# Thirteen prepared pairs, a fifth pair by seven products, and another order of DVE's and the transfers' work in an up projection

## The chip, the cores and the metric

The kernel runs on one core of one Trainium2 chip. The metric is the device time of one execution in microseconds (us); the time of a version is the median of its runs. Engines are called as in the profile: PE (TensorE's matmuls), PEld (its weight loads), DVE (VectorE), ACT (ScalarE), POOL (GpSimd), SP (SyncE, which only queues transfers here).

## The reference, cut to what matters

One decoder layer for 256 positions of width 2048: a projection, two kinds of attention (8 + 8 heads), an output projection, and an MLP with a hidden width of 8192. The change lies in the first half of the MLP.

```python
x = x + _rmsnorm(mixed @ w_out[layer], norm_attn_post[layer])
h = _rmsnorm(x, norm_mlp_pre[layer])
u = jnp.square(jax.nn.relu(h @ w_up[layer]))
x = x + _rmsnorm(u @ w_down[layer], norm_mlp_post[layer])
```

Everything is float32, `h` is 256 x 2048, `w_up` 2048 x 8192, `w_down` 8192 x 2048.

## The kernel before, in words

**Products.** A float32 operand is split into two float32r parts: `hi` (a rounded copy, by ACT, `split` L306 or with a gain L310) and `lo` (what is left, by DVE, L307 or L311). A product of two operands is three matmuls of 128 x 128 by 128 x 512 (`three`: hi·hi, hi·lo, lo·hi).

**Weights.** All weight tiles of the kernel stand in one list (`weights.plan`). A tile is 128 x 1024 at most. `weights.get(i)` emits the work on the tiles up to `i + 6`: a load by SP into one of 5 buffers `raw`, then the split into one of 8 pairs of buffers `hi` and `lo`; `weights.free(i)` gives tile `i`'s buffers back. `weights.first[i]` holds functions that are called just before tile `i` is made. So what they queue stands on its engine's queue between the work of tiles `i - 1` and `i`, some six tiles ahead of PE.

**The up projection** runs in 8 chunks `j` of 1024 columns. A chunk has 16 rows of tiles `k` (128 rows of `w_up` each). `UP_STEPS[j]` gives its order: a step `k` is one tile, 12 matmuls (2 blocks of 128 positions, 2 halves of 512 columns, 3 each). A step `p` or `w` is a pair of rows, `2k` and `2k + 1`, done as a 2 x 2 block product by Winograd's seven products in place of eight (`seven_products`): 21 matmuls and not 24. For it the weights' side needs sums of the pair's four blocks:

- In a `w` pair DVE makes them. POOL queues two transfers of the pair into the tile `ab` (`load_two`, L374), and DVE adds (`seven`: L359, L363, L364) into `t` and `u`. These additions (`sums`) are called `SUMS_AHEAD` = 2 tiles ahead of the pair's first tile, and no sooner than the last `w` pair's tiles are planned. Then four tiles are split: half of `a`, then `b`, `u`, `t`.
- In a `p` pair the sums lie in HBM, made by transfers alone while the front of the kernel runs (`prepare`, L577 to L584: two copies by SP, then four accumulating transfers by POOL; the flow below starts one pair every 24 us). They are loaded like weights, by SP into `raw`.

The left side's sums, of `hT`, are made once for each pair (`left_sums`), by DVE and ACT; with them `hT` itself gets its gain, so later chunks split these rows' weights without one (`SCALED`).

At the end of a chunk's pairs, `close` combines four accumulators `m` (PSUM banks) into four tiles `c` in SBUF: one copy by ACT (L1052), four operations by DVE (L1055). The banks of `m` are those of the next chunk's accumulators. `up_evac` then runs for each of the chunk's four quarters: DVE adds `c` to the accumulator (L954), ACT applies relu with a scale (L957), PE transposes (L300, tile `rt`), ACT squares into `uT` (L971).

**Order.** The program is emitted by hand in one order. `Flow` keeps a modelled clock that each matmul moves on by 0.216 us; generators such as `up_evac`, `left_sums` and `prepare_all` yield delays, and `flow.pump()`, called after each group of three matmuls, emits the steps that are due. Every engine works through its own part of that order. So a `yield` sets not a time but the place of an instruction in its engine's queue.

Of the kernel before, what the change touches and what calls it, by code (L numbers as in the profile page):

```python
# [18 lines left out]
F32 = mybir.dt.float32  # L19
F32R = mybir.dt.float32r  # L20
# [3 lines left out]
OP = mybir.AluOpType  # L24
PSUM = bass.MemoryType.PSUM

P = 128
# [65 lines left out]
D_UP, UP_STEP = 1.8, 2.2  # L93


SUMS_AHEAD = 2
NUP = FF // CW


def steps_of(text):  # L100

    return [(s[0], int(s[1:])) for s in text.split()]


UP_STEPS = {0: [("k", k) for k in range(KD)]}
for _j in range(1, 6):
    UP_STEPS[_j] = steps_of("k8 k9 k10 k11 p0 k12 w1 k13 w2 p3 k14 k15")
for _j in range(6, NUP):
    UP_STEPS[_j] = steps_of("k6 k7 k8 k9 k10 w0 k11 k12 w1 k13 w2 k14 k15")
SCALED = {j: range(8) for j in range(1, NUP)}  # L110
PREP = [(j, k) for j in UP_STEPS for w, k in UP_STEPS[j] if w == "p"]
D_PREP = (50.0, 24.0, 12.0)

# [53 lines left out]
class Weights:  # L167
# [15 lines left out]
    def load(self, src, w, name, queue=None):  # L183
        raw = self.pool.tile([P, CW], F32, tag="raw", bufs=RAW_BUFS, name=name)
        out = raw[:, :w]
        if len(src.shape) == 3:
            out = out.rearrange("p (k n) -> p k n", k=src.shape[1])
        (queue or self.nc.sync).dma_start(out=out, in_=src)
        return raw
# [74 lines left out]
def layer(nc, tc, io):  # L264
# [38 lines left out]
    def split(hi, lo, src, g=None):  # L303
        if g is not None:
            return split_gain(hi, lo, src, g)
        nc.scalar.activation(hi, src, AF.Copy)  # L306
        nc.vector.tensor_tensor(out=lo, in0=src, in1=hi.bitcast(F32), op=OP.subtract)  # L307
# [33 lines left out]
    def up_weight(j, k):  # L341
        return io["w_up"][k * P:(k + 1) * P, j * CW:(j + 1) * CW]
# [4 lines left out]
    def seven(load, targets):  # L347

        st, tt, H = {}, nc.vector.tensor_tensor, 512

        def sums():
            ab = load()
            a, b = st["a"], st["b"] = [ab[:, :CW], ab[:, CW:]] if not isinstance(ab, list) else ab
            t, u = st["t"], st["u"] = targets()
            if not isinstance(ab, list):
                two = [x.rearrange("p (k n) -> p k n", n=H) for x in (t, ab)]
                tt(out=two[0], in0=two[1][:, 0:2, :], in1=two[1][:, 1:4:2, :], op=OP.add)  # L359
            else:  # L360
                for x, o in ((a, 0), (b, H)):
                    tt(out=t[:, o:o + H], in0=a[:, o:o + H], in1=x[:, H:], op=OP.add)
            tt(out=u[:, :H], in0=t[:, :H], in1=b[:, H:], op=OP.add)  # L363
            tt(out=u[:, H:], in0=u[:, :H], in1=b[:, :H], op=OP.add)  # L364

        def b11(hi, lo):
            split(hi[:, :H], lo[:, :H], st["a"][:, :H])

        return sums, [b11] + [lambda hi, lo, n=n: split(hi, lo, st[n]) for n in "but"]

    def load_two(raw, queue, src):
        for i in range(2):
# [29 lines left out]
        st, left[c, kp] = down_parts(c, kp)  # L402
        nc.gpsimd.dma_start(out=st.bitcast(F32), in_=skeep[kp])

    def plan_seven(sums, fs, after, more=(), last=()):

        at = max(len(weights.specs) - SUMS_AHEAD, after)
        for n, f in (*more, (0, sums), *((0, f) for f in last)):
            weights.first.setdefault(at - n, []).append(f)
        return [weights.plan(f) for f in fs], len(weights.specs)  # L410

    wide_u, after = [], 0
    for j in range(NUP):
        wide_u.append([])
        for what, k in UP_STEPS[j]:
            if what == "k":
                g = () if k in SCALED.get(j, ()) else (gcol[:, 8 + k:9 + k],)
                ts = [weights.plan(up_weight(j, k), 1, CW, *g)]  # L420
            elif what == "p":
                kept = sums_kept[j, k]
                ts = [weights.plan(src, 1, n) for src, n in (
                    (up_weight(j, 2 * k)[:, :512], 512), (up_weight(j, 2 * k + 1), CW),
                    (kept[:, CW:], CW), (kept[:, :CW], CW))]
            else:
                ts, after = plan_seven(*seven_up(j, k), after)
            wide_u[j].append((what, k, ts))

    def down_weight(c, k):  # L430
# [518 lines left out]

    def up_evac(j, b, i, acc, order, more=None):  # L950

        yield UP_STEP * order
        if more is not None:
            nc.vector.tensor_tensor(out=acc, in0=acc, in1=more, op=OP.add)  # L954
            yield 1.6
        r = late["up"].tile([P, 512], F32, tag="r", bufs=2, name=f"r{j}_{b}")
        nc.scalar.activation(r, acc, AF.Relu, scale=rstd2[b])  # L957
        yield D_UP if j > 1 else 2 * D_UP
        t = bank(i, f"rt{j}_{b}")
        for k in range(4):  # L960
            transpose(t[:, k * P:(k + 1) * P], r[:, k * P:(k + 1) * P])
        if j not in uT:
            if j in (12, 13):
                t2 = late["ab"][:, (j - 12) * CW:(j - 11) * CW]
            elif j == 10:
                t2 = late["up"].tile([P, CW], F32, tag="uT10", bufs=1, name="uT10")
            else:
                tag = {"tag": "T", "bufs": 2} if j > 13 else {}
                t2 = late["up"].tile([P, CW], F32, name=f"uT{j}", **tag)
            uT[j] = t2.rearrange("p (k s) -> p k s", k=4)  # L970
        nc.scalar.activation(uT[j][:, :, b * P:(b + 1) * P], t.rearrange("p (k s) -> p k s", k=4), AF.Square)  # L971
# [91 lines left out]
    for j in range(FF // CW):  # L1063
        at = {bn: 4 * (j % 2) + i for i, bn in enumerate(PARTS)}
        if j == 0:
            accs = {bn: acc_bank(f"acc_u0_{bn[0]}{bn[1]}") for bn in at}
            at = {bn: (turn[0] - 3 + i) % 4 for i, bn in enumerate(at)}
        else:
            accs = {bn: bank(i, f"acc_u{j}_{bn[0]}{bn[1]}") for bn, i in at.items()}
        steps = wide_u[j]  # L1070
        order = in_order(len(steps), (APART[1], 0)) if j == 0 else [(t, b) for t, (w, _, _) in enumerate(steps)
                                                                    for b in range(NB if w == "k" else 1)]
        for t, b in order:
            what, k, tiles = steps[t]
            if (j, t, b) == (0, 8, 0):
                flow.finish(*res)
                late["po"].release()
                mix.release()
                late["up"] = pool("up", "right")
                late["st"] = late["up"].tile([P, 3 * CW], F32R, tag="st", bufs=1, name="st")  # L1080
                for n in ("ab", "c"):
                    late[n] = late["up"].tile([P, 2 * CW], F32, name=n)
                late["st2"] = late["up"].tile([P, CW], F32R, tag="uT10", bufs=1, name="st2")
                flow.start(some_sums((0, 1)))
                flow.start(some_sums((2, 3), 18.0))
            if (j, t, b) == (FF // CW - 1, 4, 0):
                weights.limit -= 1
                u_next = split_u(0, 0)
            if what != "k":
                flow.until(lambda: len(sums) > k)  # L1090
            if what == "k":
                w = weights.get(tiles[0])
                h_done(k, b)
                for n in range(2):
                    c = slice(n * 512, (n + 1) * 512)
                    three(accs[b, n], [tok(hT[x], k, b) for x in range(2)], [w[x][:, 0, c] for x in range(2)], t == 0, t == len(steps) - 1)
                    if j == 0 and t == len(steps) - 1:
                        evac.append(flow.start(up_evac(n, b, at[b, n], accs[b, n], 2 * b + n - 0.25 * (2 * b + n))))
                    flow.pump()
                if b == NB - 1:  # L1100
                    weights.free(tiles[0])
                continue

            pairs = [s[1] for s in steps if s[0] != "k"]
            first, last = k == pairs[0], k == pairs[-1]
            if first:
                m = {n: bank(i, f"m{n}_{j}") for n, i in zip((1, 6, 7, 5), free)}
            blocks = [[tok(hT[x], 2 * k + kk, bb) for x in range(2)] for kk, bb in ((0, 0), (1, 0), (1, 1))]
            seven_products(tiles, (blocks, sums[k]), accs, m, first, last)
            if last:  # L1110
                more = close(closing(), m)
        free = [at[bn] for bn in PARTS]
        if j:
            for o, (b, n) in enumerate(PARTS):
                evac.append(flow.start(up_evac(2 * j + n, b, at[b, n], accs[b, n], o + 0.1, more[b, n])))
    u_last = evac[-4:]
    up = late["up"]

# [195 lines left out]
```

## Time and profile before

| what | value |
|---|---|
| median of 3 runs | 1063.76 us (1063.56 to 1064.2) |
| profiled execution, its own time | 1066.42 us |
| its span, first to last instruction | 1064.6 us |
| mean granted clock of PE | 0.997 |
| bytes moved by DMA | 260.81 MB |
| up projection, from its first matmul to the down projection's first | 355.8 to 719.5 us of the span |
| chunks 1 to 7 begin at about | 403, 447, 494, 539, 584, 630, 676 us |

The page of the profile gives, for each engine, how long it was busy; a PE that is shown as busy is not always at its peak, since matmuls overlap. The queries behind it give the waits (which engine stood idle until which other one), the busy time in windows, and the instructions in order of time. Idle time of an engine that is not the bottleneck costs nothing by itself.

### The profile page before, as it was taken

Reading aid. Unit: us, or ns where it says so; the run is one execution under the profiler, and the core shown is the slowest. Engines: PE = TensorE matmul, PEld = TensorE weight load, DVE = VectorE, ACT = ScalarE, POOL = GpSimd, SP = SyncE. Lnnn points to the kernel's source line nnn. Section 1 sums busy time; section 2 is a strip of 40 time slices with the busy share of each in tenths; the row PEclk is TensorE's granted clock in tenths of the full one; section 3 lists DMA queues with packets and bytes.
Section 4 is the critical chain, followed back from the end, with each engine's and each line's share of the span. In section 5 each row is a group of like instructions: output and inputs, shape, how many; then the busy total and the mean of one; then the engine's idle time right before and its main releaser. Section 6 shows DMA issues by size and latency. Waiting matters only on the chain.

```text
span 1064.6 us, 13618 instructions
## 1 busy us (share of the span) xinstructions
PE 1041.5 (98%) x4839; PEld 863.4 (81%) x4839; DVE 811.2 (76%) x1083; ACT 631.1 (59%) x846; POOL 94.5 (9%) x148
## 2 busy tenths in 40 slices
PE   9999999999999999999999999999999999999996
PEld 6888899888888788777878778888888888888885
DVE  6666546577556678878788798988799978989995
ACT  6574436566454566565665657666566664766761
POOL 0011111112001000000000000001000001122100
PEclk9999999999999999999999999999999999999998
DMA  9999879699887285748676484469688867788952
GB/s 309 350 297 289 212 200 328 201 268 278 236 230 235 95 310 188 254 155 283 201 229 223 160 286 166 157 221 325 233 296 280 279 239 250 283 302 294 372 202 81
DMA packets 94724, 260.81 MB, mean 245 GB/s; under 512 B 8896, under 2 KB 13504, under 8 KB 94272
## 3 DMA queue, kind: packets, MB, share of 16 engines
q1 hardware_dynamic: 74080, 199.00, 54.3%
q0 software_dynamic: 20000, 60.30, 21.0%
q8 instruction: 38, 0.62, 0.2%
q10 hardware_dynamic: 576, 0.64, 0.2%
q14 instruction: 30, 0.25, 0.1%
HBM read 244.18 MB, written 39.32 MB: 266 GB/s over the span
## 4 chain that ended last, share of the span: by engine, by line
PE 72%; DVE 12%; DMA 8%; issue 4%; ACT 3%; DVEq 0%; POOL 0%; POOLq 0%; ACTq 0%; SPq 0%
PE y L296 25%; PE acc_o L296 8%; PE acc_u L296 6%; PE md L296 5%; PE acc_qk L296 4%; DVE lo L307 4%; PE acc_v L296 4%; DMA raw<-in_w_up 4%; PE acc_ckv L296 2%; DVE lo L311 2%; DMA ab<-in_w_up 2%; PE acc_ukv L296 2%; PE acc_q L296 2%; PE acc_cq L296 2%; PE acc_k L296 2%
## 5 line engine op out<-in xcount | busy, mean ns | idle before, releaser
L307 DVE TENSOR_TENSOR lo<-raw,hi 128x1024 fp32r<-128x1024 f32 (+3 forms) x257 | 288.0, 1142 | 96.5 <-ACT hi L306 95.8
L306 ACT ACTIVATE hi<-raw 128x1024 fp32r<-128x1024 f32 (+3 forms) x257 | 250.8, 992 | 101.4 <-PE y L296 20.8
L296 PE MATMUL y<-hi,uhi 128*128 128x512 f32 x376 | 146.6, 390 | 0.0
L296 PE MATMUL y<-hi,ulo 128*128 128x512 f32 x376 | 146.4, 389 | 0.0
L296 PE MATMUL y<-lo,uhi 128*128 128x512 f32 x376 | 146.3, 389 | 0.0
L296 PE MATMUL acc_u<-hi,hT_hi 128*128 128x512 f32 x356 | 142.4, 400 | 3.6 <-DVE c L1055 3.5
L296 PE MATMUL acc_u<-lo,hT_hi 128*128 128x512 f32 x356 | 139.1, 391 | 0.8 <-DVE lo L311 0.8
L296 PE MATMUL acc_u<-hi,hT_lo 128*128 128x512 f32 x356 | 139.2, 391 | 0.4 <-DVE hT_lo L307 0.4
L311 DVE SCALAR_TENSOR_TENSOR lo<-raw,gcol,hi 128x1024 fp32r<-128x1024 f32 x72 | 91.8, 1281 | 27.1 <-ACT hi L310 26.6
L310 ACT ACTIVATE hi<-raw,gcol 128x1024 fp32r<-128x1024 f32 x72 | 82.5, 1149 | 32.8 <-DMA raw<-in_w_up 18.3
L296 PEld LDWEIGHTS y<-lo,uhi 128*128 128x128 f32 x376 | 70.6, 188 | 14.7
L296 PEld LDWEIGHTS y<-hi,ulo 128*128 128x128 f32 x376 | 70.6, 188 | 14.6
L296 PEld LDWEIGHTS y<-hi,uhi 128*128 128x128 f32 x376 | 70.6, 188 | 14.5
L296 PEld LDWEIGHTS acc_u<-hi,hT_hi 128*128 128x128 f32 x356 | 66.9, 188 | 18.8 <-DVE c L1055 6.2
L296 PEld LDWEIGHTS acc_u<-hi,hT_lo 128*128 128x128 f32 x356 | 66.8, 188 | 15.1 <-DVE hT_lo L307 0.8
L296 PEld LDWEIGHTS acc_u<-lo,hT_hi 128*128 128x128 f32 x356 | 67.0, 188 | 14.0 <-DVE lo L311 1.2
L296 PE MATMUL m<-hi,st 128*128 128x512 f32 x156 | 56.5, 389 | 0.0
L296 PE MATMUL acc_o<-hi,mixT_hi 128*128 128x512 f32 x128 | 51.8, 405 | 0.0
L307 DVE TENSOR_TENSOR lo<-st_down,hi 128x1024 fp32r<-128x1024 f32 x40 | 48.0, 1220 | 4.0 <-ACT hi L306 3.8
L296 PE MATMUL acc_o<-hi,mixT_lo 128*128 128x512 f32 x128 | 50.2, 392 | 0.0
L296 PE MATMUL acc_o<-lo,mixT_hi 128*128 128x512 f32 x128 | 50.0, 390 | 0.0
L306 ACT ACTIVATE hi<-st_down 128x1024 fp32r<-128x1024 f32 x40 | 42.1, 1052 | 11.1 <-PE y L296 9.5
(326 smaller groups left out, 2000.8 us busy)
## 6 DMA issues: line engine op xcount, KB each, us to landing
raw<-in_w_down SPq DMA_DIRECT2D x88, 512.0 KB, 5.9
raw<-in_w_up SPq DMA_DIRECT2D x86, 512.0 KB, 5.0
raw<-in_w_in SPq DMA_DIRECT2D x55, 512.0 KB, 6.2
raw<-in_w_out SPq DMA_DIRECT2D x32, 512.0 KB, 7.5
ab<-in_w_up POOLq DMA_DIRECT2D x28, 512.0 KB, 4.9
sums<-in_w_up SPq DMA_DIRECT2D x20, 512.0 KB, 7.2
raw<-sums SPq DMA_DIRECT2D x20, 512.0 KB, 3.9
ab_down<-in_w_down POOLq DMA_DIRECT2D x20, 512.0 KB, 6.7
```

The source lines that it names most:

```text
L296: nc.tensor.matmul(out, a, b, start=start, stop=stop)
L306: nc.scalar.activation(hi, src, AF.Copy)
L307: nc.vector.tensor_tensor(out=lo, in0=src, in1=hi.bitcast(F32), op=OP.subtract)
L310: nc.scalar.activation(hi, src, AF.Copy, scale=g)
L311: nc.vector.scalar_tensor_tensor(out=lo, in0=src, scalar=g, in1=hi.bitcast(F32), op0=OP.mult, op1=OP.subtract)
```

## The change

It does the following in the up projection:

- chunks 2 to 4 have the pairs 0 to 4 as seven products (three `p`, two `w`) in the order `k10 k11 k12 p0 w1 p2 k13 w3 p4 k14 k15`; chunks 1 and 5 keep four pairs, in the order `p0 k12 w1 k13 p2 w3`. So 13 pairs are prepared in HBM, where there were 10. A fifth set of left sums is made in chunk 1; from chunk 2 on the rows 8 and 9 of `hT` hold their gain.
- the prepared sums of chunks 1 to 4 are loaded by one transfer of 1 MB on POOL's queue into a new tile `tu`, up to 6 tiles ahead and not before the last `p` pair's tiles are planned; the splits read `tu`. Chunk 5 loads its sums as before. `tu` later becomes the place of `uT8` and `uT9`, and the longer `st2` that of `uT10` and `uT11`.
- the loads of `ab` are called up to `LOAD_AHEAD` = 3 tiles ahead of the additions (not before the third tile of the last `w` pair), apart from the last chunk's second and third pair.
- in `up_evac` the addition L954 is the first step; a quarter's chain begins as soon as that quarter's last matmuls are emitted, and the quarters' relus are 0.75 x 2.2 us apart and not 2.2.

```diff
-SUMS_AHEAD = 2
+SUMS_AHEAD, LOAD_AHEAD = 2, 3
...
-for _j in range(1, 6):
-    UP_STEPS[_j] = steps_of("k8 k9 k10 k11 p0 k12 w1 k13 w2 p3 k14 k15")
+UP_STEPS[1] = UP_STEPS[5] = steps_of("k8 k9 k10 k11 p0 k12 w1 k13 p2 w3 k14 k15")
+for _j in range(2, 5):
+    UP_STEPS[_j] = steps_of("k10 k11 k12 p0 w1 p2 k13 w3 p4 k14 k15")
...
-SCALED = {j: range(8) for j in range(1, NUP)}
+SCALED = {j: range(8 if j == 1 else 10) for j in range(1, NUP)}
...
-            ab = load()
+            ab = st["ab"] if "ab" in st else load()
...
+        def early():
+            st["ab"] = load()
+
-        return sums, [b11] + [lambda hi, lo, n=n: split(hi, lo, st[n]) for n in "but"]
+        return sums, [b11] + [lambda hi, lo, n=n: split(hi, lo, st[n]) for n in "but"], early
...
-    def plan_seven(sums, fs, after, more=(), last=()):
+    def plan_seven(sums, fs, early, after, more=(), last=(), soon=False):
 
         at = max(len(weights.specs) - SUMS_AHEAD, after)
+        if soon:
+            more = (*more, (at - max(at - LOAD_AHEAD, after - 2), early))
...
+                if j < 5:
+                    at = max(len(weights.specs) - 2 * LOAD_AHEAD, after_p)
+                    weights.first.setdefault(at, []).append(
+                        lambda kept=kept: nc.gpsimd.dma_start(out=late["tu"], in_=kept))
+                    ts = [weights.plan(src, 1, n) for src, n in srcs[:2]] + [weights.plan(
+                        lambda hi, lo, o=o: split(hi, lo, late["tu"][:, o:o + CW])) for o in (CW, 0)]
+                    after_p = len(weights.specs)
+                else:
+                    ts = [weights.plan(src, 1, n) for src, n in srcs]
             else:
-                ts, after = plan_seven(*seven_up(j, k), after)
+                ts, after = plan_seven(*seven_up(j, k), after, soon=j < NUP - 1 or k == 0)
...
+        if more is not None:
+            yield 0.2
+            nc.vector.tensor_tensor(out=acc, in0=acc, in1=more, op=OP.add)
+            yield 1.4
         yield UP_STEP * order
-        if more is not None:
-            nc.vector.tensor_tensor(out=acc, in0=acc, in1=more, op=OP.add)
-            yield 1.6
...
+            if (j, t, b) == (1, 4, 0):
+                flow.start(some_sums((4,), 6.0))
...
-                    if j == 0 and t == len(steps) - 1:
-                        evac.append(flow.start(up_evac(n, b, at[b, n], accs[b, n], 2 * b + n - 0.25 * (2 * b + n))))
+                    if t == len(steps) - 1:
+                        evac.append(flow.start(up_evac(2 * j + n, b, at[b, n], accs[b, n], 0.75 * (2 * b + n),
+                                                       more[b, n] if j else None)))
...
-        if j:
-            for o, (b, n) in enumerate(PARTS):
-                evac.append(flow.start(up_evac(2 * j + n, b, at[b, n], accs[b, n], o + 0.1, more[b, n])))
```

More of the change, by code (lines that the diff above doesn't have):

```diff
@@ L410, in plan_seven @@
         return [weights.plan(f) for f in fs], len(weights.specs)
-    wide_u, after = [], 0
+    wide_u, after, after_p = [], 0, 0
     for j in range(NUP):
@@ L422, in layer @@
                 kept = sums_kept[j, k]
-                ts = [weights.plan(src, 1, n) for src, n in (
-                    (up_weight(j, 2 * k)[:, :512], 512), (up_weight(j, 2 * k + 1), CW),
-                    (kept[:, CW:], CW), (kept[:, :CW], CW))]
+                srcs = [(up_weight(j, 2 * k)[:, :512], 512), (up_weight(j, 2 * k + 1), CW),
+                        (kept[:, CW:], CW), (kept[:, :CW], CW)]
+                if j < 5:
[7 more added lines that the diff above has]
+                    ts = [weights.plan(src, 1, n) for src, n in srcs]
             else:
-                ts, after = plan_seven(*seven_up(j, k), after)
+                ts, after = plan_seven(*seven_up(j, k), after, soon=j < NUP - 1 or k == 0)
             wide_u[j].append((what, k, ts))
@@ L964, in up_evac @@
                 t2 = late["ab"][:, (j - 12) * CW:(j - 11) * CW]
-            elif j == 10:
-                t2 = late["up"].tile([P, CW], F32, tag="uT10", bufs=1, name="uT10")
+            elif j in (8, 9):
+                if j == 8:
+                    late["uT8"] = late["up"].tile([P, 2 * CW], F32, tag="uT8", bufs=1, name="uT8")
+                t2 = late["uT8"][:, (j - 8) * CW:(j - 7) * CW]
+            elif j in (10, 11):
+                if j == 10:
+                    late["uT10"] = late["up"].tile([P, 2 * CW], F32, tag="uT10", bufs=1, name="uT10")
+                t2 = late["uT10"][:, (j - 10) * CW:(j - 9) * CW]
             else:
@@ L1082, in layer @@
                     late[n] = late["up"].tile([P, 2 * CW], F32, name=n)
-                late["st2"] = late["up"].tile([P, CW], F32R, tag="uT10", bufs=1, name="st2")
+                late["st2"] = late["up"].tile([P, 2 * CW], F32R, tag="uT10", bufs=1, name="st2")
+                late["tu"] = late["up"].tile([P, 2 * CW], F32, tag="uT8", bufs=1, name="tu")
                 flow.start(some_sums((0, 1)))
                 flow.start(some_sums((2, 3), 18.0))
+            if (j, t, b) == (1, 4, 0):
+                flow.start(some_sums((4,), 6.0))
             if (j, t, b) == (FF // CW - 1, 4, 0):
```

## The prediction

> **What bounds the kernel now.** The first view is the page's table of busy time, the second a table of windows that cuts the span at the stages.
>
> ```profile
> PE 1041.5 (98%) x4839; PEld 863.4 (81%) x4839; DVE 811.2 (76%) x1083; ACT 631.1 (59%) x846; POOL 94.5 (9%) x148
> ```
>
> ```profile
> core 0: us, PE busy (x) PEld busy (x) DVE busy (x) ACT busy (x) POOL busy (x), PEclk, DMA share, GB/s
> 0.00:355.80 355.80, 353.74 (x1754) 299.64 (x1755) 217.40 (x403) 197.60 (x336) 42.88 (x53) 1.00 0.88 257
> 402.00:450.00 48.00, 45.97 (x209) 37.37 (x209) 42.46 (x53) 30.28 (x38) 2.15 (x4) 1.00 0.67 218
> 450.00:495.00 45.00, 42.72 (x195) 34.66 (x194) 35.74 (x38) 28.30 (x33) 2.15 (x4) 1.00 0.66 222
> 675.00:720.00 45.00, 45.00 (x208) 37.25 (x207) 38.89 (x43) 27.57 (x32) 0.02 (x1) 1.00 0.52 173
> 720.00:1050.00 330.00, 330.00 (x1465) 273.33 (x1464) 285.65 (x328) 202.06 (x226) 33.26 (x62) 1.00 0.77 270
> ```
>
> TensorE is the bound, at the full granted clock. The front and the down projection leave it nothing to wait for; what it loses lies in the up projection, between 402 and 675, chunks 1 to 5. The third view, the waits of PE from 340 to 725, names the losses, and the waits of DVE and ACT (395 to 725) what lies behind them.
>
> ```profile
> PE rt L300 <- ACT r L957: 7.7, 6, 1.6
> PE acc_u L296 <- DVE c L1055: 3.5, 3, 1.3
> PE acc_u L296 <- DVE lo L311: 0.8, 1, 0.8
> ```
>
> ```profile
> DVE t L359 <- DMA ab<-in_w_up: 14.8, 6, 3.0
> ```
>
> ```profile
> ACT r L957 <- DVE acc_u L954: 28.6, 15, 6.0
> ACT hi L310 <- DMA raw<-in_w_up: 12.4, 10, 4.6
> ACT hi L306 <- DMA raw<-sums: 12.2, 8, 2.9
> ```
>
> PE waits 12.0 us in 10 places: for the transposes of a finished chunk (its relu waits for the addition L954), for the closing of the seven products (L1055, which frees the banks of the next accumulators), and once for a split. A matmul is shown as 0.39 us but they start every 0.227 us, so each wait costs about 0.16 us more than its row: 12.0 + 10 x 0.16 = 13.6 us. All are waits for DVE, which itself stands 14.8 us for `ab`, six times.
>
> **The change, part by part.**
>
> *Matmuls.* A pair by two ordinary steps takes 24, by seven products 21. Chunks 2, 3 and 4 get a fifth pair: 9 fewer.
>
> ```profile
> 714.24 5.44 PE acc_u L296 x24
> ```
>
> At 5.44 / 24 = 0.227 us that is -2.0 us, on the bound engine. Chunks 1 and 5 only change the order and kind of their pairs: 0.
>
> *DVE work.* By form, from 395 to 725:
>
> ```profile
> L311 DVE SCALAR_TENSOR_TENSOR lo<-raw,gcol,hi 128x1024 fp32r<-128x1024 f32 x55 | 70.2, 1281 | 16.8 <-ACT hi L310 16.3
> L307 DVE TENSOR_TENSOR lo<-raw,hi 128x1024 fp32r<-128x1024 f32 x42 | 49.8, 1218 | 4.0 <-ACT hi L306 4.0
> L307 DVE TENSOR_TENSOR lo<-raw,hi 128x512 fp32r<-128x512 f32 x10 | 6.8, 682 | 0.0
> ```
>
> A prepared pair is one split of 0.68 and three of 1.22, 4.3 us; the two plain tiles that it replaces are 2 x 1.28 = 2.6. So DVE gets 1.8 us more in each of chunks 2 to 4: about 36 + 1.8 = 38 us, for a chunk of PE work of some 42 (177 x 0.227 = 40.2, and four transposes of about 0.36). Chunk 7 shows that it can carry this: 38.9 us in 45 and no wait of PE. With the 2 to 3 us of waits left at each boundary (below) DVE keeps about 5 us in hand. Price 0; if that cover is gone, each us over it costs PE one. Leaving the gain out of the splits of k8 and k9 in chunks 5 to 7 saves 0.06 us each: nothing. ACT, at 28 of 45, stays under.
>
> *The fifth left sums* (`some_sums((4,))`) are added to chunk 1, DVE's fullest (42.5 of 48). The timeline has the first and last of the eight instructions of one set:
>
> ```profile
> 413.40 0.68 DVE L1010 TENSOR_TENSOR c<-hT_hi,hT_lo 128x512 f32<-128x512 f32 x1
> 415.77 1.28 DVE L311 SCALAR_TENSOR_TENSOR lo<-raw,gcol,hi 128x1024 fp32r<-128x1024 f32 x1
> 417.56 0.68 DVE L1021 TENSOR_TENSOR st<-c,st 128x512 fp32r<-128x512 f32 x1
> ```
>
> 2.4 us up to the split, 1.2 behind it: +3.6 us of DVE. Against it the wait for `ab` in this chunk goes:
>
> ```profile
> 425.25 1.23 DVE L359 TENSOR_TENSOR t<-ab 128x1024 f32<-128x1024 f32 x1 [3.00 <-DMA ab<-in_w_up]
> ```
>
> Even, then: the lead of the splits stays as thin as it is. For the wait for a split (0.8 + 0.16) I keep 0.5.
>
> *Loads.* `ab` is requested up to three tiles ahead of the additions, at the earliest when the last pair's own splits of `ab` are queued. The sums of 11 pairs come over POOL's queue as 1 MB into `tu` and no longer as two loads on SP's, so in chunks 2 to 4 the five raw buffers serve 6 + 3 x 2 = 12 loads and not 8 + 2 x 4 = 16, and plain tiles run further ahead.
>
> ```profile
> raw<-in_w_up SPq DMA_DIRECT2D x65, 512.0 KB, 4.8
> ab<-in_w_up POOLq DMA_DIRECT2D x26, 512.0 KB, 4.8
> ```
>
> 1 MB lands between 4.8 (as one) and 9.6 us (as two in a row); `tu` of a second or third pair is asked for six tiles before its first split, some 10 us of PE. I take the 14.8 us of DVE's waits as gone but for 2 or 3 us a chunk, inside the 5 in hand. Queued behind such a wait on POOL is only the next `ab`.
>
> *Additions.* This decides. In the flow's clock (0.216 us a matmul, groups of three) the first quarter's transposes now come four groups into the next chunk, 12 matmuls or 2.7 us; before they came eight groups in, 24 matmuls. The DVE and PE timelines of the boundary from chunk 2 to 3 (rows in order of time, PE between DVE):
>
> ```profile
> 488.47 0.39 PE L296 MATMUL acc_u<-hi,hT_hi 128*128 128x512 f32 x1
> 493.91 0.39 PE L296 MATMUL acc_u<-hi,hT_hi 128*128 128x512 f32 x1
> 499.69 0.60 PE L300 MATMUL rt<-ident,r 128*128 128x128 f32 x4
> ```
>
> ```profile
> 492.39 2.28 DVE L1055 TENSOR_TENSOR c<-m,c 128x512 f32<-128x512 f32 x3
> 495.30 2.95 DVE L307 TENSOR_TENSOR lo<-raw,hi 128x512 fp32r<-128x512 f32 x3
> 498.17 0.69 DVE L954 TENSOR_TENSOR acc_u<-acc_u,c 128x512 f32<-128x512 f32 x1
> 498.77 1.21 DVE L359 TENSOR_TENSOR t<-ab 128x1024 f32<-128x1024 f32 x1
> 501.36 1.22 DVE L307 TENSOR_TENSOR lo<-raw,hi 128x1024 fp32r<-128x1024 f32 x1
> ```
>
> Products end at T = 488.47, the chunk at T + 5.44. Closing lasts 2.9 (492.39 to 495.30), additions of a pair 2.6 (498.77 to 501.36). In the new order of chunks 2 to 4 the first w pair stands at tiles 7 to 10, so its additions are queued with tile 5, at the step k15 of the chunk before, ahead of the L954 of that chunk. DVE then runs: closing (done at about T + 4.0), split 1.14, additions 2.6, split 1.14, L954 0.69; ACT's relu 0.69 and 0.1 of signalling make T + 10.3. The transposes are due at T + 5.44 + 2.72 = T + 8.2. So PE waits 2.2 us at each of the boundaries into chunks 3 and 4, about what it waits now (rt and c together). Into chunk 5 the additions are queued behind L954: 0 (now 2.6 to 3). Closing by T + 4.0 is within its cover (5.44 + 1.36 to the third quarter's bank), so the c waits go.
>
> Into chunk 2 DVE is late now (closing begins 5 us after the products' end) and will be as late:
>
> ```profile
> 446.53 2.28 DVE L1055 TENSOR_TENSOR c<-m,c 128x512 f32<-128x512 f32 x3
> 453.21 0.69 DVE L954 TENSOR_TENSOR acc_u<-acc_u,c 128x512 f32<-128x512 f32 x1
> ```
>
> With the additions ahead of L954, 2.6 us more before it, and transposes due earlier: I take 4.8 (now 4.1 with c). Into chunk 6 the additions of w0 are queued before the closing, as now: 1.2 (now 2.7). Into chunk 7, now free of waits, L954 is shown 3.1 us after the chunk's start:
>
> ```profile
> 676.12 0.39 PE L296 MATMUL acc_u<-hi,hT_hi 128*128 128x512 f32 x1
> 677.44 1.82 DVE L307 TENSOR_TENSOR lo<-ab,hi 128x512 fp32r<-128x512 f32 x2
> ```
>
> After the first of these splits (0.6) come L954 and the relu, 679.5; transposes are due at 676.12 + 2.72 = 678.8: a new wait of 0.6. Sum: 0.5 + 4.8 + 2.2 + 2.2 + 0 + 1.2 + 0.6 = 11.5, against 13.6: -2.1 us. Bounds: the boundaries into 3 and 4 cannot go under some 1.5 each (a closing at T + 3.5), nor the lag into 2 under 2; so the gain is at most 13.6 - 5 = 8.6. The other way the waits may stay at 13.6 or grow by the new ones, +2.
>
> *Preparation.* Three more pairs follow the ten:
>
> ```profile
> L577 SPq DMA_DIRECT2D sums<-in_w_up x10: 522/522/612, 52.9 to 283.9; - x10
> L584 POOL DMA_DIRECT2D sums<-sums x10: 1156/1172/1197, 74.7 to 322.8; - x10
> ```
>
> One takes (283.9 - 52.9) / 9 = 25.7 us, so the last three of thirteen run to about 400; in the order of the list they are those of chunks 4 and 5, wanted after 540. On POOL's queue they share with `rstd_post` and `rstd_pre`:
>
> ```profile
> 363.51 0.55 POOL L504 TENSOR_TENSOR rstd_post<-t_post,neg_half 128x1 f32<-128x1 f32 x1 [12.76 <-DVE t_post L503]
> ```
>
> The last transfer that the new pairs queue ahead of this one (L584 of the eleventh) follows the tenth's, 322.8, by one period: 348.5. The row's start is 363.5, with 12.8 us of idle POOL ahead of it: cover enough, and 10 us more would have to go wrong before the norm is late. SP gets 2 x 3 issues of 0.5 to 0.6 us. Their bytes meet the loads of 369 to 388, when every engine of the DMA is busy; PE shows no wait there. I take 0, bounds -0.3 (noise of landing) and +3.
>
> **Sum.** -2.0 - 2.1 + 0 = -4.1 us. The profiled execution took 1066.42 us with a span of 1064.6; the median of the runs, 1063.76, is what the forecast is for: 1059.6 us.
>
> **The rivals.** *B, the additions are hidden.* If DVE is early enough at each boundary, the waits fall to the lower bound above: -2.0 - 8.6, 1053.2. For it: chunks 6 and 7 carry the same load with no wait. Against: DVE works in order, and 2.6 us stand ahead of L954. 0.12.
>
> *C, waits only move.* They stay at 13.6 or gain 1: about 1062.3. For it: the waits at the boundaries into 3 and 4 come out as now by my count. 0.17.
>
> *D, slower: what POOL brings comes late.* `tu` has one buffer and stands in one queue with `ab`: a transfer waits for the last splits of the pair before, and `ab` behind it. Two of each a chunk; if each makes DVE wait 2.4 us more than I think (9.6 a chunk), the 5 in hand are passed by 4.6, thrice: 13.8 - 4.1, or 1073.5. The gain is used up from 5 + 4.1 / 3 = 6.4 us a chunk, and at 7.1 the time is 1066. Against it: POOL's loads land as soon as SP's, 4.8 us. The Trainium skill, page "SBUF — State Buffer", section "SBUF: two separate sides", says that a DMA from POOL's queue cannot get its descriptors written while VectorE is in a two-port mode, which speaks against moving the sums off SP's queue. By that rule D would come; the 4.8 us beside a DVE that is busy four fifths of the time do not show it, and the same page of the Trainium skill, section "Who interferes with whom", gives `tensor_tensor`, most of DVE's work here, no such mode. 0.13.
>
> **How the numbers follow.** The forecast (A) has 0.58 and its own range is 1056.5 to 1061.5. Faster by more than 0.2% (2.1 us, about what a measurement of this kernel can tell) are A and B: 0.70; C is the same: 0.17; D slower: 0.13. B at 1053 and D beyond 1065 are each about a tenth, so the range is 1055 to 1064.5.
>
> **What would show it.** Right: 4830 matmuls; L359's waits for `ab` mostly gone; PE's wait for c gone; its wait for r still 8 to 11 us, the longest into chunk 2, with L954 directly behind L364 and a split on DVE. Wrong: r waits under 4 us (B), a new wait of ACT or DVE for `tu` above 10 us or PE waits for splits in chunks 2 to 4 (D), waits of PE between 360 and 400 (preparation).

## The result, and the profile after

The changed kernel takes 1079.18 us (median of 4 runs, 1076.6 to 1081.47) against 1063.98 us before: ratio 1.0142, 95% interval 1.0117 to 1.0166. The forecast was 1059.6 us. The profiled execution took 1079.97 us. The first lines of its page and its table of windows:

```profile
span 1078.2 us, 13612 instructions
...
PE 1046.0 (97%) x4830; PEld 867.8 (80%) x4830; DVE 818.0 (76%) x1097; ACT 637.1 (59%) x854; POOL 110.9 (10%) x171
```

```profile
0.00:355.80 355.80, 353.65 (x1755) 299.71 (x1756) 217.72 (x403) 197.78 (x337) 46.49 (x57) 1.00 0.91 266
355.80:402.00 46.20, 43.94 (x199) 34.25 (x198) 24.40 (x35) 22.75 (x37) 10.12 (x13) 1.00 0.83 259
402.00:450.00 48.00, 41.82 (x182) 33.95 (x181) 46.16 (x67) 36.02 (x45) 4.44 (x7) 0.93 0.72 244
450.00:495.00 45.00, 40.46 (x175) 32.91 (x174) 37.62 (x41) 26.03 (x32) 2.36 (x5) 0.92 0.61 202
675.00:720.00 45.00, 44.61 (x205) 36.67 (x204) 39.37 (x44) 27.84 (x33) 0.05 (x1) 1.00 0.55 177
720.00:1050.00 330.00, 330.00 (x1465) 273.24 (x1464) 289.51 (x328) 207.57 (x231) 32.84 (x62) 1.00 0.80 278
```

The nine matmuls are gone, and front and down projection are as they were. The loss lies between 356 and 585, and two columns show it: PE is busy less, and PEclk, which was 1.00 everywhere, falls to 0.93 and 0.92 between 402 and 495, and to 0.96 in the next two windows, up to 585. From 355.8 to 402 PE was busy 45.8 us before the change and is busy 43.9 now; the row of before:

```profile
355.80:402.00 46.20, 45.80 (x213) 37.47 (x212) 35.16 (x51) 30.75 (x47) 3.25 (x5) 1.00 0.68 244
```

The waits of PE and of ACT from 340 to 725, after the change:

```profile
PE rt L301 <- ACT r L972: 19.0, 6, 5.7
PE acc_u L297 <- DVE lo L312: 2.2, 3, 0.8
```

```profile
ACT hi L311 <- DMA raw<-in_w_up: 22.5, 10, 6.5
ACT r L972 <- DVE acc_u L968: 22.0, 5, 5.4
ACT hi L307 <- DMA raw<-in_w_up: 17.6, 9, 4.3
ACT hi L307 <- DMA tu<-sums: 4.9, 3, 1.8
```

(L972 is the relu, L968 the addition, L1076 the closing, L301 the transposes.) The waits for the closing are gone, the waits for the relu have grown from 7.7 to 19.0 us. Measured from matmul start to matmul start, PE's waits of 340 to 735 were 14.3 us before and are 23.4 now; another 6.3 us or so are some 30 matmuls that start every 0.427 us instead of every 0.227. With the nine matmuls (-2.0) that makes 9.1 + 6.3 - 2.0 = 13.4 us; the spans of the two profiled executions differ by 13.6, the medians by 15.2. The 23.4 are: splits at 368 to 404 3.4 (0.6 of it the kernel before has too); the transposes at the boundary into chunk 1 5.8, into chunk 2 4.7, into 3 4.1, into 4 4.3, into 5 none, into 6 and 7 0.6 each.

### The profile page after: what moved, and what is told of

It is laid out like the page before. It is cut to its first block, busy times and chain, and to the rows that moved or that the text cites. A ratio compares the mean times of both kernels' runs of the same rounds, so it can differ in the third digit from the quotient of the medians.

```text
span 1078.2 us, 13612 instructions
## 1 busy us (share of the span) xinstructions
PE 1046.0 (97%) x4830; PEld 867.8 (80%) x4830; DVE 818.0 (76%) x1097; ACT 637.1 (59%) x854; POOL 110.9 (10%) x171
## 4 chain that ended last, share of the span: by engine, by line
PE 81%; DVE 9%; DMA 5%; issue 3%; ACT 1%; POOL 0%; DVEq 0%; POOLq 0%; ACTq 0%
PE y L297 25%; PE acc_u L297 13%; PE acc_o L297 8%; PE md L297 5%; DMA raw<-in_w_up 4%; PE acc_qk L297 4%; PE acc_v L297 4%; PE m L297 4%; DVE lo L308 4%; PE acc_ckv L297 2%; PE acc_ukv L297 2%; PE acc_q L297 2%; PE acc_cq L297 2%; PE acc_k L297 2%; DVE lo L312 2%
## 5 line engine op out<-in xcount | busy, mean ns | idle before, releaser
L308 DVE TENSOR_TENSOR lo<-raw,hi 128x1024 fp32r<-128x1024 f32 (+3 forms) x253 | 282.4, 1134 | 102.9 <-ACT hi L307 102.2
L307 ACT ACTIVATE hi<-raw 128x1024 fp32r<-128x1024 f32 (+3 forms) x253 | 245.9, 986 | 112.1 <-PE y L297 21.8
L297 PE MATMUL acc_u<-hi,hT_hi 128*128 128x512 f32 x338 | 137.5, 407 | 0.0
L297 PE MATMUL acc_u<-lo,hT_hi 128*128 128x512 f32 x338 | 134.9, 399 | 2.4 <-DVE lo L312 2.2
L297 PE MATMUL acc_u<-hi,hT_lo 128*128 128x512 f32 x338 | 134.7, 399 | 0.4 <-DVE hT_lo L308 0.4
L312 DVE SCALAR_TENSOR_TENSOR lo<-raw,gcol,hi 128x1024 fp32r<-128x1024 f32 x60 | 75.5, 1280 | 24.7 <-ACT hi L311 24.3
L311 ACT ACTIVATE hi<-raw,gcol 128x1024 fp32r<-128x1024 f32 x60 | 68.1, 1148 | 27.7 <-DMA raw<-in_w_up 23.6
L297 PEld LDWEIGHTS acc_u<-hi,hT_hi 128*128 128x128 f32 x338 | 64.9, 192 | 13.4 <-ACT hi L311 0.7
L297 PE MATMUL m<-hi,st 128*128 128x512 f32 x174 | 63.0, 389 | 0.0
```

The source lines that it names most:

```text
L297: nc.tensor.matmul(out, a, b, start=start, stop=stop)
L311: nc.scalar.activation(hi, src, AF.Copy, scale=g)
L312: nc.vector.scalar_tensor_tensor(out=lo, in0=src, scalar=g, in1=hi.bitcast(F32), op0=OP.mult, op1=OP.subtract)
```

## The experiments

Each run was made beside the kernel before, and its ratio is to that. An "own" pair is a `w` pair, whose sums DVE makes, a "prepared" one a `p` pair. "T" is the start of the first matmul behind a chunk's last product. Theory T1, formed from the trace: the late preparations crowd the loads around 390 us; the next pair's additions hold up the transposes; long waits halve the clock.

**The preparations and the additions.** Four edits of the changed kernel:

```diff
e1  -D_PREP = (50.0, 24.0, 12.0)
    +D_PREP = (50.0, 19.0, 9.0)
e2  (first own pair of chunks 2 to 4; the place of early() stays)
    +        at += later
    +                                       later=int(k == 1 and 2 <= j <= 4))
e4  -    UP_STEPS[_j] = steps_of("k10 k11 k12 p0 w1 p2 k13 w3 p4 k14 k15")
    +    UP_STEPS[_j] = UP_STEPS[1]
    (and no fifth left sums)
```

> The changed kernel with the thirteen preparations 19 us apart on the plan's clock instead of 24, so that the last one is issued before the norm's loads instead of among them. Theory T1 (the last preparations crowd the loads of 367 to 407 us): the waits for splits there (3.4 us), the wait of 5.8 us before the transposes of chunk 0 and the half clock behind it (about 2.4 us) go: 1079.2 - 11.6 = 1067.6 us. Rival R1 (the loads are late by themselves, or the fifth left sums are what holds the VectorE up there): no change beyond 2 us, 1077 to 1081 us.

> The changed kernel with the additions of the first VectorE-made pair of chunks 2, 3 and 4 queued one tile later, behind three of the four additions into the accumulators instead of ahead of all four. T1 (these 2.6 us of additions hold the transposes up): the waits of 4.7, 4.1 and 4.3 us at the boundaries into chunks 2, 3 and 4 become 2.0, 1.5 and 1.6, and with no wait of over 4 us there the half clock behind them (about 4.4 us) goes too: 1079.2 - 8.0 - 4.4 = 1066.8 us. Rival R2 (the half clock has another cause than the long waits): 1079.2 - 8.0 = 1071 us, the clock's rows stay. Rival D (VectorE has no time in hand): the pair's own blocks are late instead, waits for splits of 6 us or more, 1077 us or more.

> Both edits, the preparations 19 us apart and the additions one tile later. T1: 1079.2 - 11.6 - 12.4 = 1055 us, the granted clock at 1.00 through the up projection. If the two losses share a cause, one edit brings most of what both bring: 1064 us or more.

> The changed kernel with chunks 2 to 4 as chunk 1 is (four pairs, two of them prepared, ten preparations in all, no fifth left sums); the early loads, the transfers of the right sums into a tile and the additions queued at once stay. T1: the nine matmuls return (+2.0 us), the preparations end where they ended before, the additions of the next pair stand 24 matmuls ahead of the transposes: waits of the up projection about 2 us instead of the 13.6 of the kernel before, 1064.0 - 11.6 = 1052.4 us, no half clock. Rival R3 (the early queueing of the additions, or the loads further ahead, is what costs): 1070 us or more, with the transposes' waits still there.

| run | us | ratio to before |
|---|---|---|
| e1 | 1069.2 | 1.0038 (1.0021 to 1.0056) |
| e2 | 1064.8 | 0.9999 (0.9986 to 1.0011) |
| e1 and e2 | 1057.3 | 0.9930 (0.9909 to 0.9951) |
| e4 | 1051.2 | 0.9871 (0.9853 to 0.9888) |

T1's times hold in all four, within 2.5 us. Its full clock in the run with both edits does not: there the clock still fell once, behind waits of 1.1 and 2.1 us. In e1 the wait into chunk 1 is gone and those into 2, 3 and 4 stay (4.7, 3.5, 4.3); in e2 it is the other way round: 6.9 into chunk 1, then 1.2, 1.6 and 1.4. The windows of e2 say the same of the clock: half speed only where the long wait is left.

```profile
402.00:450.00 48.00, 40.75 (x177) 33.43 (x178) 46.22 (x66) 34.85 (x43) 4.42 (x7) 0.93 0.75 254
450.00:495.00 45.00, 43.94 (x202) 36.11 (x202) 41.37 (x44) 29.73 (x35) 3.68 (x7) 1.00 0.68 233
495.00:540.00 45.00, 43.53 (x200) 35.80 (x199) 37.85 (x40) 29.72 (x35) 3.68 (x7) 1.00 0.69 254
```

The transfers alone were then put on top of e4, with sums that nobody reads:

```diff
e8  -PREP = [(j, k) for j in UP_STEPS for w, k in UP_STEPS[j] if w == "p"]
    +PREP = [(j, k) for j in UP_STEPS for w, k in UP_STEPS[j] if w == "p"] + [(j, 1) for j in (2, 3, 4)]
```

> The run with four pairs, with three more preparations, 24 us apart behind the ten, whose sums nobody reads. Only the transfers are added. T1 (their bytes crowd the loads of 350 to 407 us): the waits for splits and at the end of chunk 0 come back with the half clock behind them, 1051.2 + 11 = 1062 us. Rival R1 (it was the fifth left sums or the additions, not the transfers): 1050 to 1053 us.

1063.3 us (ratio 0.9986, 0.9977 to 0.9995): +12.0 on e4, with a wait of 6.1 us into chunk 1 and half clock behind it. R1 is out. The DMA issues of 367 to 407, first of the kernel before, then of e4, of the changed kernel and of e8 (KB each, median us to landing):

```profile
raw<-in_w_up SPq DMA_DIRECT2D x15, 512.0 KB, 6.3
```

```profile
raw<-in_w_up SPq DMA_DIRECT2D x17, 512.0 KB, 6.7
```

```profile
DMA  0053999999999999999999999999999999999999
...
raw<-in_w_up SPq DMA_DIRECT2D x13, 512.0 KB, 13.3
sums<-in_w_up POOLq DMA_DIRECT2D x6, 256.0 KB, 12.2
ab<-in_w_up POOLq DMA_DIRECT2D x2, 512.0 KB, 16.3
```

```profile
raw<-in_w_up SPq DMA_DIRECT2D x13, 512.0 KB, 12.0
```

The DMA was busy here in e4, too, and in the kernel before; with the late pairs' transfers among them the same load takes twice as long. ACT then waits for the bytes of chunk 0's last tiles and of those behind them (four times, 1.3 to 6.5 us, up to 406), and DVE waits with it. The left sums stand between these splits on both queues, and the first relu of chunk 0, behind all of them on ACT's, starts at 414.0; in e4 it starts at 401.3.

**Which part of the change is worth what.** e4 is 14 us faster than the kernel before, with the same matmuls. Its parts:

```diff
e5  the kernel before with the changed up_evac and its place in the loop, no other part
e6  e4 with up_evac and its place as in the kernel before
e11 the kernel before, one line:
    -    UP_STEPS[_j] = steps_of("k8 k9 k10 k11 p0 k12 w1 k13 w2 p3 k14 k15")
    +    UP_STEPS[_j] = steps_of("k8 k9 k10 k11 p0 k12 w1 k13 p2 w3 k14 k15")
e14 e4 with this line undone
```

> The kernel before with one part of the change alone: the additions into the accumulators queued at once behind the chunk's last products, instead of an instalment each between later steps. From the run with four pairs, whose gain in the up projection over the kernel before is 14.0 us. T1: this part brings most of it, since the transposes and not the loads were what the TensorE waited for: 1064 - 10 = 1054 us, the waits for c gone. Rival R4 (the waits of the VectorE for ab hold the boundaries): within 3 us of the kernel before, 1061 to 1064 us.

> The run with four pairs with the additions queued as in the kernel before: it keeps the early loads of ab, the right sums' own tile and the new order of the pairs. T1: 1064 - 4 = 1060 us. Rival R4: 1055 us or less. If the two parts only work together, both this run and the one before are at 1062 us or more.

> The kernel before with one edit: chunks 1 to 5 in the order ... w1 k13 p2 w3 k14 k15 instead of ... w1 k13 w2 p3 k14 k15, so that a pair made by the VectorE is the last one. No other part of the change. T2: the closings start at 0.3 to 1.5 us instead of 3.9 to 6.5, most of the 14 us between the kernel before and the run with four pairs come from this: 1053 to 1057 us. Rival R5 (the early loads of ab, or the right sums' own tile, do it): 1061 to 1065 us.

> The run with four pairs with one edit undone: chunks 1 to 5 in the order of the kernel before (... w1 k13 w2 p3 k14 k15, a prepared pair last). It keeps the early loads, the right sums' own tile and the additions queued at once. T2 (the order is what brings the gain; the tile takes two of the four raw buffers' turns off the last pair): closings at 2 to 3 us, waits of 1.5 to 3 us at each of five boundaries, 1051.2 + 9 = 1060 us. Rival R5 (the rest would have brought it too): 1050 to 1054 us.

| | additions, loads, tile as before | additions at once only | all three new |
|---|---|---|---|
| prepared pair last | 1064 to 1065 (before) | e5 1059.3: 0.9948 (0.9932 to 0.9965) | e14 1069.9: 1.0048 (1.0032 to 1.0065) |
| own pair last | e11 1049.3: 0.9845 (0.9830 to 0.9860) | not run | e4 1051.2: 0.9871 (0.9853 to 0.9888) |

e6 has the early loads and the tile with the additions as before, and an own pair last: 1051.0, ratio 0.9872 (0.9857 to 0.9888). So my T1 was wrong on e5 and e6 (rival R4 was right on e6 and missed e5 by 2 us): the additions at once bring 5.7 us where a prepared pair is last and nothing where an own pair is. T2, formed after the run e7 (below), had e11 and its sign right, though e11 came out 4 us under the range, and e14 came out 10 us worse than it said. One swapped pair is the whole gain, and the early loads with the tile on top of the additions cost 10.6 us in the old order (e14 against e5; the loads and the tile were not run apart). e11 is the fastest of all runs, faster than both kernels; its waits of PE from 340 to 740 are one row:

```profile
PE acc_u L296 <- DVE hT_lo L307: 0.4, 1, 0.4
```

The boundary into chunk 3 on ACT's timeline shows how. The kernel before (T = 488.47):

```profile
487.42 3.73 ACT L310 ACTIVATE hi<-raw,gcol 128x1024 fp32r<-128x1024 f32 x3 [0.95 <-DMA raw<-in_w_up]
491.05 0.57 ACT L1052 ACTIVATE c<-m 128x512 f32<-128x512 f32 x1
```

The changed kernel (T = 501.46), e14 (T = 490.94) and e11 (T = 483.01):

```profile
503.22 0.63 ACT L307 ACTIVATE hi<-raw 128x512 fp32r<-128x512 f32 x1 [4.12 <-DMA raw<-in_w_up]
503.75 0.58 ACT L1073 ACTIVATE c<-m 128x512 f32<-128x512 f32 x1
```

```profile
493.95 1.15 ACT L311 ACTIVATE hi<-raw,gcol 128x1024 fp32r<-128x1024 f32 x1 [5.38 <-DMA raw<-in_w_up]
495.01 0.58 ACT L1073 ACTIVATE c<-m 128x512 f32<-128x512 f32 x1
```

```profile
481.02 1.15 ACT L310 ACTIVATE hi<-raw,gcol 128x1024 fp32r<-128x1024 f32 x1 [0.37 <-DVE lo L311]
482.08 0.57 ACT L1052 ACTIVATE c<-m 128x512 f32<-128x512 f32 x1
```

The closing's first step, the copy `c<-m`, is queued behind the split of a tile of the *next* chunk, six tiles ahead. In the first three that tile's bytes are not there, for two reasons. In the kernel before the prepared pair's four loads have just held the raw buffers, and the five loads behind them go out one after the other between T - 8.9 and T - 4.3; in e11, where the last pair reads `ab`, four of these five went out at T - 11.9 or sooner. In the changed kernel and e14 the late tile's load goes out at T - 5.8 and T - 5.5, no later than in e11 (T - 5.7), but among 2 MB of early loads: `tu` is free only when the prepared pair that is last has been split, so its next load is issued at T - 6.7 and T - 6.5, and those of `ab`, behind it on POOL's queue, within about 1 us after. In e4, with an own pair last, `tu` goes out at T - 12.0 and `ab` at T - 11.4. The DMA's lines around T of e14 (482 to 494; GB/s in 40 slices of 0.3 us), then the loads of e11 around its T (474 to 486):

```profile
GB/s 55 164 273 437 437 341 369 355 396 355 96 41 287 0 109 137 410 355 410 437 410 437 410 382 423 369 423 423 437 396 410 423 403 396 464 403 389 396 458 389
...
raw<-in_w_up SPq DMA_DIRECT2D x5, 512.0 KB, 9.3
tu<-sums POOLq DMA_DIRECT2D x1, 1024.0 KB, 6.8
ab<-in_w_up POOLq DMA_DIRECT2D x2, 512.0 KB, 9.7
```

```profile
raw<-in_w_up SPq DMA_DIRECT2D x3, 512.0 KB, 4.2
```

The transfers bunch at some 400 GB/s, and the raw loads land in 9.3 us instead of 4.2. The start of the closing on DVE behind T, by the trace of each run (us):

| run | last pair of 1; 2 to 4 | chunk 1 | 2 | 3 | 4 |
|---|---|---|---|---|---|
| before | prepared; prepared | 5.2 | 3.9 | 3.9 | 4.0 |
| changed | own; prepared | 3.8 | 3.0 | 3.2 | 0.3 |
| e14 | prepared; prepared | 6.0 | 5.4 | 5.6 | 0.3 |
| e4 | own; own | 2.7 | 0.4 | 0.7 | 0.3 |
| e11 | own; own | 1.9 | 0.4 | 0.4 | 0.4 |

Chunk 4's column is a control inside two runs: chunk 5 does not use the tile `tu`, so `ab` is not held up on POOL's queue either (it goes out at T - 14.2), and with a prepared pair last the closing still starts at 0.3.

The swap of e11 did one thing more: DVE's waits for `ab` from 395 to 725 fell from 14.8 us to 2.0, without any early load. By themselves such waits do not make the closing late: in e14's chunk 4 DVE waits 1.8 us for `ab`, at 564, and that closing starts at 0.3. Whether they had a share in the late closings of the kernel before, beside the late bytes, was not run apart.

**Can the fifth pair be kept?** Six more edits of the changed kernel, with the preparations 20 us apart:

```diff
e7  "k10 k11 k12 k13 p0 w1 p2 w3 p4 k14 k15"
e10 e7, and W_AHEAD 5 instead of 6
e9  "k10 k11 k12 k13 p0 w1 p2 p3 w4 k14 k15"
e9b "k10 k11 k12 p0 w1 p2 k13 p3 w4 k14 k15", and e2's edit
e13 e9, and:  -                if j < 5:
              +                if j < 5 and k != 3:
e15 e9, with no early loads, no tile tu, and up_evac as in the kernel before
```

> The changed kernel, all five pairs of chunks 2 to 4 kept, with k13 moved ahead of the first pair (so 24 matmuls, not 12, lie between the chunk's last products and the point where the next pair's additions are due) and the preparations 20 us apart. T1: no wait of over 1 us at the boundaries, the nine matmuls (2.0 us) come on top of the gain of the run with four pairs, and the closer preparations cost about 1 us in the attention: 1051.2 - 2.0 + 1 = 1050 us. Rival D (five pairs in one row give the VectorE no tile of the lighter kind between them): waits for splits of 5 us or more in chunks 2 to 4, 1055 us or more.

> The run with k13 ahead of the first pair, with tiles split five ahead instead of six. T2: the split with the late bytes is then queued behind the closing instead of ahead of it; the closings start at about 1.5 us instead of 5.3, the waits for c and most of the transposes' waits (9 us of the 11.4) go: 1059.4 - 9 = 1050 us. R6: nothing gained, or worse for the shorter look-ahead, 1058 us or more.

> The changed kernel with chunks 2 to 4 in the order k10 k11 k12 k13 p0 w1 p2 p3 w4 k14 k15 (still five pairs, three of them prepared, but the last pair is one that the VectorE adds itself, which takes no raw buffers) and the preparations 20 us apart. Theory T2, formed from the run with k13 ahead of the first pair: with a prepared pair last, two more raw buffers of five are taken just before the closing, the tile that is split ahead of it gets its bytes late, and the closing starts 3 to 5.5 us behind the last product instead of 0.3. T2: the closings into chunks 3, 4 and 5 start at 0.3 to 1 us, no wait for c, transposes never late there: 1051.2 - 2.0 + 1 = 1050 us. Rival R6 (five pairs simply fill the VectorE): waits as in the run with k13 ahead, 1057 us or more; the second load of the right sums' tile in a row could add waits for splits of about 2 us per chunk, 1056 us.

> The same with the order k10 k11 k12 p0 w1 p2 k13 p3 w4 k14 k15, the additions of the first VectorE-made pair one tile later, preparations 20 us apart. T2: closings at 0.3 to 1 us, the accumulators' additions done before the transposes are due, 1050 us. R6: 1056 us or more.

> The five-pair order with an own pair last (k10 k11 k12 k13 p0 w1 p2 p3 w4 k14 k15, preparations 20 us apart), with the right sums of p3 loaded through the raw buffers, as the kernel before does, instead of through the one tile that p2 has just used. In the run without this edit the VectorE stood 3.5 us for that tile's second load and was 4.7 us behind from there to the closing. T3 (that stall is what ate the five pairs' gain there): the closings start at 0.5 to 1.5 us instead of 5.2 to 6.2, the waits for c (1.5 us, four times) and of the transposes go: 1066 - 12 to 14 = 1052 to 1054 us. Rival R6 (five pairs fill the VectorE whatever the order): 1062 us or more.

> Five pairs in chunks 2 to 4 in the order k10 k11 k12 k13 p0 w1 p2 p3 w4 k14 k15, preparations 20 us apart, and nothing else of the change: no early loads of ab, the right sums through the raw buffers, the additions spread as in the kernel before. T4, from the two by two (the early loads and the tile's loads meet the raw buffers' loads just ahead of the closing): closings at 0.3 to 1.5 us, 1049.3 - 2.0 + 1 = 1048 us. Rival R6 (five pairs leave the VectorE no room for an own pair early in the chunk): 1052 us or more.

| run | us | ratio to before | closing behind T, chunks 1 to 4 |
|---|---|---|---|
| e7 | 1059.4 | 0.9948 (0.9931 to 0.9966) | 5.4, 5.3, 5.5, 2.5 |
| e10 | 1076.1 | 1.0085 (1.0055 to 1.0115) | 3.0, 3.0, 2.0, 2.1 |
| e9 | 1066.0 | 1.0012 (0.9999 to 1.0026) | 5.2, 6.2, 5.7, 5.6 |
| e9b | 1081.2 | 1.0141 (1.0119 to 1.0163) | 4.6, 2.9, 1.4, 4.5 |
| e13 | 1054.6 | 0.9903 (0.9888 to 0.9918) | 5.3, 2.5, 2.6, 2.3 |
| e15 | 1059.9 | 0.9952 (0.9937 to 0.9966) | 5.2, 3.3, 3.1, 3.7 |

None of my forecasts of 1048 to 1050 us (e7, e10, e9, e9b, e15) was reached. In e10 the closings did come up to 3.5 us earlier, but the shorter look-ahead holds for the down projection as well, which lost some 22 us (start of the last 1000 matmuls to the end); its waits of PE from 740 to 1060 begin with

```profile
PE y L297 <- DVE lo L308: 13.3, 5, 5.8
```

In e9 two prepared pairs in a row share the one tile `tu`; ACT's timeline has the stall, and with it DVE is late at the closing although an own pair is last. So T2's "own pair last" is not enough by itself.

```profile
475.42 2.01 ACT L307 ACTIVATE hi<-tu 128x1024 fp32r<-128x1024 f32 x2 [6.22 <-DMA tu<-sums]
```

e13 takes that stall away and gains 11.4 us on e9. T3's time, 1052 to 1054, was missed by 0.6 us only, but its closings at 0.5 to 1.5 us did not come: those into chunks 3 to 5 start at 2.3 to 2.6. T4 failed in e15, which has neither early loads nor the tile and an own pair last: at its boundary into chunk 3 (T = 488.06) the split ahead of the copy waits for its bytes again, since its load goes out at T - 3.5 only, in e11 at T - 5.7. What frees that buffer late was not found, so R6 stays open.

```profile
488.99 1.15 ACT L311 ACTIVATE hi<-raw,gcol 128x1024 fp32r<-128x1024 f32 x1 [3.01 <-DMA raw<-in_w_up]
```

In e9b the additions stood up to 11.5 us for `ab`, and PE 18.8 us for splits of its pairs. The closing of chunk 1, in which the fifth left sums are made, starts at 4.6 to 5.4 us in these runs (e10 3.0), against 2.7 and 1.9 in e4 and e11, which have chunk 1's order without them; the left sums were not run apart. The best run with five pairs, e13, is 3.4 us slower than e4, which has nine matmuls more. That DVE has no room for a fifth pair in any order is not shown; what is shown is that no run with five pairs was as fast as e4 or e11.

## Why the prediction was wrong, point by point

Against the forecast of -4.1 us the waits came out 11.3 us larger (23.4, less the 0.6 that the forecast left out before and after, against 11.5), and the clock cost 6.3: +13.5, where the spans differ by 13.6. The steps:

- *Matmuls*, -2.0: right, 4830.
- *Preparation*, 0 with bounds -0.3 and +3: this step failed first. The last of the transfers went out at 406.6 us, as worked out ("to about 400"), and the norm's chain had its cover. But "their bytes meet the loads of 369 to 388 ... PE shows no wait there" took the missing wait for room; raw loads went from 6.3 to 13.3 us, DVE fell behind, and PE paid at the end of chunk 0. Measured: 10.0 us (e1) to 12.0 (e8), half clock included. The named sign, waits between 360 and 400, appeared.
- *The boundaries into chunks 3 and 4*, 2.2 each: measured 4.1 and 4.3. The order on DVE was right (closing, split, additions of 2.6, split, addition), and e2 showed its price: without those additions the waits are 1.6 and 1.4. The closing failed: "done at about T + 4.0" was T + 6.0, because the tile split ahead of it had no bytes. The row of the kernel before had it done at T + 6.8, and the working has no step for the 2.8 us less. DVE's timeline there:

```profile
503.88 0.69 DVE L308 TENSOR_TENSOR lo<-raw,hi 128x512 fp32r<-128x512 f32 x1 [3.31 <-ACT hi L307]
504.49 2.27 DVE L1076 TENSOR_TENSOR c<-m,c 128x512 f32<-128x512 f32 x3
506.80 0.69 DVE L1076 TENSOR_TENSOR c<-c,m 128x512 f32<-128x512 f32 x1
507.40 1.22 DVE L308 TENSOR_TENSOR lo<-raw,hi 128x1024 fp32r<-128x1024 f32 x1
508.54 1.22 DVE L360 TENSOR_TENSOR t<-ab 128x1024 f32<-128x1024 f32 x1
512.26 1.89 DVE L968 TENSOR_TENSOR acc_u<-acc_u,c 128x512 f32<-128x512 f32 x3
```

- *Loads*: the step said that the early loads take DVE's waits for `ab` away, and they did:

```profile
DVE t L360 <- DMA ab<-in_w_up: 2.4, 1, 2.4
```

  That they would push the raw loads back was not asked. "Queued behind such a wait on POOL is only the next `ab`" named the queue, and missed whom its transfers meet. I had quoted ACT's 12.4 us of waits for `raw` before and did not ask what stood behind them: the closing.
- *Boundaries into 2, 5, 6, 7*: 4.8, 0, 1.2, 0.6 forecast; 4.7, 0, 0.6, 0.6 measured. The match into 2 is partly luck: the 4.8 was taken and not summed, and the closing that was to begin 5 us behind T began at 3.8.
- *The fifth left sums*, "even, then": open. Chunk 1's closing is later in the runs that have them, but the wait into chunk 2 came out as forecast.
- *The clock*: no term for it; some 6.3 us.
- *Rivals B and C* had the wrong sign: the waits neither fell nor stayed.
- *Rival D* had the sign and the queue but not the mechanism: ACT waited 4.9 us for `tu`, DVE 2.4 for `ab`, and PE for no split of chunks 2 to 4. The rule of the Trainium skill, page "SBUF — State Buffer", section "SBUF: two separate sides" (POOL's transfers held up while VectorE is in a two-port mode), did not show here; since most of DVE's work has no such mode, as the prediction said, this is no real test of it. `tu`'s transfers landed beside a busy DVE in 5.2 us:

```profile
tu<-sums POOLq DMA_DIRECT2D x11, 1024.0 KB, 5.2
```

## What to carry to other kernels

When a step is priced at "hidden", look at the resource and not only at the waits: a DMA that is full may have no room left though nothing waits for it (here transfers that nobody reads cost 12 us). Before an operation that frees something (here the closing), list what stands ahead of it on its engine and where the bytes of that come from; a prefetch queued there can cost more than it saves, and swapping two pairs gained 15.7 us where the whole change lost 15.2. And a wait that grows past two us may be paid twice, by itself and by the clock after it.

## What the runs showed of the hardware

The granted clock after a wait. The changed kernel around the boundary into chunk 2:

```profile
460.00:463.40 3.40, 0.52 (x3) 0.09 (x1) 3.33 (x4) 0.00 (x0) 0.00 (x0) 1.00 0.65 198
463.40:470.40 7.00, 5.34 (x16) 4.37 (x17) 4.50 (x7) 2.38 (x4) 1.06 (x2) 0.51 0.29 96
470.40:474.00 3.60, 3.60 (x21) 2.98 (x20) 1.12 (x1) 2.87 (x5) 0.00 (x0) 1.00 0.62 250
```

In the up projection half clock came after every wait of 3.5 us or more, after one of 2.56 (e15) and after two of about 1 and 2.1 us within 5 us (e1 with e2, e9b). In e14 it came after one of 2.24 us:

```profile
426.00:430.40 4.40, 2.45 (x11) 1.69 (x9) 3.73 (x5) 2.07 (x3) 0.00 (x0) 1.00 0.38 151
430.40:433.80 3.40, 3.27 (x8) 2.60 (x9) 3.40 (x5) 3.40 (x5) 0.00 (x0) 0.50 0.50 154
433.80:437.00 3.20, 3.20 (x16) 2.63 (x15) 3.20 (x4) 2.13 (x4) 0.00 (x0) 0.99 0.30 49
```

It did not come after 2.28 and 2.06 (e15), nor after pairs of 1.5 and 1.6 (e7, e9). It lasted about 3.4 or 6.8 us (once 10.2), and cost 0.2 us for each matmul started in it.

The clock records of the traces show a rule that fits all of these. Within a run all changes of the clock lie whole multiples of 3.41 us apart (in the changed kernel at 412.4, 419.2, 463.6, 470.4, 514.8, 518.2, 562.5 and 566.0). Cut on this grid, the 17 traces have 1930 stretches of 3.41 us at full clock between 340 and 735 us. In 16 of them PE was busy 1.48 us or less, and in the stretch behind each the clock was half; in the other 1914 it was busy 1.54 us or more, and the clock stayed. So what counts is how much of a wait falls into one stretch. In e15 most of the wait of 2.56 us lies in one (first row; half clock from 455.1), while the wait of 2.28 begins in the stretch before the second row:

```profile
451.70:455.10 3.40, 1.37 (x7) 0.79 (x5) 3.37 (x5) 0.61 (x2) 0.00 (x0) 1.00 0.58 210
499.50:502.90 3.40, 1.68 (x10) 1.46 (x11) 3.28 (x5) 1.37 (x3) 0.00 (x0) 1.00 0.55 171
```

This is read off the busy times of these traces, in which the ends of matmuls are modelled.

The Trainium skill, page "TensorE: Matmul & The Clock Gate", section "HAM oscillation — how this bites in real kernels", warns of idle gaps over some 3.4 us; here the clock also fell after gaps of 2.2 to 2.6 us, and the measurement decides.
